# Layer 1's lead maxima: from six after each gate product, in three banks, to four ahead of each half of one, in four banks

## The chip, the cores and the metric

The kernel runs on one core of one Trainium2 chip. The metric is the device time of one execution in microseconds; the number compared is the median over runs.

## The reference

Two layers act on 1024 latent tokens and 256 context tokens with model width 1024. Layer 0 is grouped-query attention, layer 1 is multi-head latent attention with 16 heads. Each layer projects its input, attends, multiplies the result by a gate and projects back. The change touches layer 1 alone, in which the context tokens give keys but no output:

```python
def mla_attend(q_nope, q_rope, k_nope, k_rope, v):
    s = (jnp.einsum('bqhd,bkhd->bhqk', q_nope, k_nope)
         + jnp.einsum('bqhr,bkr->bhqk', q_rope, k_rope)).astype(jnp.float32) * ((MLA_NOPE + MLA_ROPE) ** -0.5)
    p = jax.nn.softmax(s, axis=-1).astype(v.dtype)
    return jnp.einsum('bhqk,bkhd->bqhd', p, v)
...
    o = sweep_query_blocks(lambda qn, qr: mla_attend(qn, qr, kn_all, kr_all, v_all), q_nope, q_rope)
    y = (o.reshape(B, S, MLA_WIDTH) * jax.nn.silu(g)) @ p["w_out"]
```

`g`, the gate, is 1024 columns of the product `h @ w_in`. A softmax needs, for each query, the maximum of its scores (or a number near it) before the exponentials are taken.

## The kernel before

All products run on TensorE in 32-bit floats, with each operand split in a high and a low part, so that one product is three matmuls (`mm3`: lines 94, 95 and 96).

**The gate slices.** The gate is made transposed, in slices of 128 columns by 512 tokens (`gate_slice`). A slice is 8 steps of the contraction times 3, so 24 matmuls of 128x512 into one bank of PSUM (a tile `mm` of the pool `ps_mm`, which has four). ScalarE then takes a tanh of the bank into a tile `gth` (line 303; the pool `wkg1` has two such tiles), VectorE makes the gate of both (line 304), and SyncE stores it to DRAM (line 305, `sgd<-gth`). The last eight slices of layer 1 stand in a loop of their own just ahead of the attention. They are called slices 0 to 7 here; slice 7 is made as two halves of 256 tokens.

**The maxima.** A unit is one head. For a unit the kernel computes, from the high parts alone, the scores of each 128 queries against 512 latent keys (kind `lat`, 16 to a unit) or of twice 128 queries against the 256 context keys (kind `ctx`, 4 to a unit). Each of these 20 steps takes one bank of PSUM (tile `mx`), which VectorE reduces to a row maximum in `m` (lines 394 and 403). TensorE uses 64 of its 128 rows for such a product: queries 0 to 511 of a head and a copy of its keys lie on partitions 0 to 63 (half 0), queries 512 to 1023 on partitions 64 to 127 (half 1). A `lat` step is two matmuls of 64x512, `KH,QH` and `KR,QR` (line 392); a `ctx` step is four of 64x256 (line 402). The list of steps alternates between the halves, and `side_by_side` issues the parts of two steps in turn. After a unit's 20th step `do_shift` takes the maximum of its three (line 450), and a "turn" transposes it on TensorE (line 459), copies it to `crow` (VectorE, line 461) and sends it by DMA into a row of `QS`, which is an operand of the unit's scores.

**The lead.** Attention's loop (`run`) issues two maxima steps with each tile of scores, but the first 24 are to be there before it starts: all 20 of unit 0 and 4 of unit 1. They are issued in the loop of the gate slices, six after each of the slices 3, 4, 5 and 6. `start_unit` issues the loads of a head (`KH`, `QH`, `QR`, then `KL`, `QL`, `QS`) on SyncE's one queue, on which the stores of the gate stand too.

**What sets the order.** Around these slices a scheduler orders TensorE's instructions. It may move a maximum among the matmuls of a slice that stands later. In `run` the order is that of the code (`manual_schedule`). VectorE, ScalarE, GpSimdE and SyncE are ordered by the scheduler in the loop of the slices, before and after the change; each then runs its list strictly in that order. The `mx` tiles come from a pool `ps_m` of three banks, which is opened before the loop and stays through the attention.

```python
            if 2 < at.step < len(todo_g) - 1:
                at.maxima(at.done + 6, 2)
            at.step += 1
            at.run_turns()
```

Of the kernel before, what the change touches and what calls it, by code (L numbers as in the profile page):

```python
# [10 lines left out]
F32 = mybir.dt.float32  # L11
# [4 lines left out]
AX = mybir.AxisListType  # L16
PSUM = bass.MemoryType.PSUM
DRAM = bass.MemoryType.DRAM

P = 128  # L20
D = 1024
KT = D // P
# [6 lines left out]
HALVES = (True, True)  # L29
WIDE = (True, False)  # L30
# [7 lines left out]
def hybrid_kernel(ctx: ExitStack, tc: tile.TileContext, ins: dict, out: bass.AP):  # L38
    nc = tc.nc
    pe, act, dve, pool, sp = nc.tensor, nc.scalar, nc.vector, nc.gpsimd, nc.sync  # L40
# [49 lines left out]
    def mm3(ps, lh, ll, rh, rl, ks, first=True, last=True, between=None):  # L90

        ks = list(ks)
        for i, k in enumerate(ks):
            pe.matmul(ps, lhsT=lh(k), rhs=rh(k), start=first and i == 0, stop=False)  # L94
            pe.matmul(ps, lhsT=lh(k), rhs=rl(k), start=False, stop=False)  # L95
            pe.matmul(ps, lhsT=ll(k), rhs=rh(k), start=False, stop=last and i == len(ks) - 1)  # L96
            if between is not None:
                between(i)
# [192 lines left out]
            pad(tiles, 96)  # L291
        return tiles.tile([P, KT, n], F32R, name="hh"), tiles.tile([P, KT, n], F32R, name="hl")

    def gate_slice(l, c, m, s0, n, w, hT, ps_mm, wk):

        hh, hl = hT[0 if s0 < NL else 1]
        hs = slice(s0 % NL, s0 % NL + n)
        ms = slice(m * P, (m + 1) * P)
        ps = ps_mm.tile([P, 512], F32, name="mm", tag="mm")
        mm3(ps[:, :n], lambda k: w[0][:, k, ms], lambda k: w[1][:, k, ms],  # L300
            lambda k: hh[:, k, hs], lambda k: hl[:, k, hs], range(KT))
        th = wk.tile([P, 512], F32, name="gth", tag="w512")
        act.activation(th[:, :n], ps[:, :n], AF.Tanh, scale=0.5)
        dve.scalar_tensor_tensor(th[:, :n], th[:, :n], 1.0, ps[:, :n], op0=ALU.add, op1=ALU.mult)  # L304
        sp.dma_start(sgd[l][4 * c + m, :, s0:s0 + n], th[:, :n])
# [4 lines left out]
    class Attention:  # L310
# [15 lines left out]
        def open_early(self, st):  # L326

            l = self.l
            self.kp = st.enter_context(tc.tile_pool(name=f"kp{l}", bufs=self.ops["kbufs"], side="right", reuse_waits="tile"))
            self.qp = st.enter_context(tc.tile_pool(name=f"qp{l}", bufs=self.ops["qbufs"], side="right", reuse_waits="tile"))  # L330
            self.ps_m = st.enter_context(tc.tile_pool(name=f"psm{l}", bufs=2 if WIDE[l] or not HALVES[l] else 3, space=PSUM, side="right", reuse_waits="tile"))
            if HALVES[l]:
                self.ops["open"](self, st)

        def open_late(self, st, stp):
            l = self.l
# [36 lines left out]
                              rhs=s["mk"][:, NL:NT], start=True, stop=True)  # L373
                dve.reduce_max(s["m"][:, 2 * i:2 * i + 2, 2 if u["kind"] == "lat" else 0], m.rearrange("p (a b) -> p a b", a=2), axis=AX.X)

        def max_parts(self, u, step):

            s = self.state[id(u)]
            kind, i, n = step
            if kind == "lat":  # L380
                half, spans = i // 4, [(i % 4, slice(n * 512, n * 512 + 512), slice(0, 512))]
            else:
                half, spans = i // 2, [(2 * (i % 2) + a, slice(NL, NT), slice(a * 256, a * 256 + 256)) for a in range(2)]
            held = {}

            def part(j):
                if j == 0:
                    held["m"] = self.ps_m.tile([P, 512], F32, name="mx", tag="mx")
                pairs = self.ops["maxima"](s, half)
                q, k = pairs[j]  # L390
                for t, ks, cs in spans:
                    pe.matmul(held["m"][:, cs], lhsT=q[:, t * P:(t + 1) * P], rhs=k[:, ks], start=j == 0, stop=j == len(pairs) - 1)  # L392
                if j == len(pairs) - 1:
                    dve.reduce_max(s["m"][:, i, n:n + 1], held["m"], axis=AX.X)  # L394

            def part_ctx():
                held["m"] = self.ps_m.tile([P, 512], F32, name="mx", tag="mx")
                m = held["m"]
                pairs = self.ops["maxima"](s, half)
                for t, ks, cs in spans:  # L400
                    for j, (q, k) in enumerate(pairs):
                        pe.matmul(m[:, cs], lhsT=q[:, t * P:(t + 1) * P], rhs=k[:, ks], start=j == 0, stop=j == len(pairs) - 1)  # L402
                dve.reduce_max(s["m"][:, 2 * i:2 * i + 2, 2 if u["kind"] == "lat" else 0],
                               m.rearrange("p (a b) -> p a b", a=2), axis=AX.X)

            if kind == "ctx":
                return half, [part_ctx] + [lambda: None] * (self.ops["mparts"] - 1)
            return half, [lambda j=j: part(j) for j in range(self.ops["mparts"])]

        def wide_max(self, u, step):  # L410
# [78 lines left out]
                self.todo += [(u, ("ctx", i, 0)) for i in range(4)]  # L489
            self.started += 1  # L490

        def next_maxima(self, upto, limit):

            steps = []
            while self.done < upto:
                if not self.todo and self.started < min(limit, len(self.units)):
                    self.start_unit()
                if not self.todo:
                    break
                u, m = self.todo.pop(0)  # L500
                self.done += 1
                if WIDE[self.l]:
                    steps += enumerate(self.wide_max(u, m))
                    continue
                half, parts = self.max_parts(u, m)
                if m[:2] == ("ctx", 3):
                    parts.append(lambda u=u: self.do_shift(u))
                steps.append((half, parts))
            return steps
# [9 lines left out]
        def maxima(self, upto, limit):  # L519

            if HALVES[self.l]:
                steps = self.next_maxima(upto, limit)
                self.side_by_side(*([f for half, parts in steps if half == a for f in parts] for a in range(2)))
                return
            while self.done < upto:
                if not self.todo and self.started < min(limit, len(self.units)):
                    self.start_unit()
                if not self.todo:
                    break
                u, m = self.todo.pop(0)  # L530
                self.done += 1
                self.do_max(u, m)
                if m[:2] == ("ctx", 3):
                    self.do_shift(u)
# [320 lines left out]
    ps_mm = stP.enter_context(tc.tile_pool(name="psmm0", bufs=4, space=PSUM, reuse_waits="tile"))  # L855
# [3 lines left out]
    right = dict(side="right", reuse_waits="tile")  # L859
    lat = st0.enter_context(tc.tile_pool(name="hlat0", bufs=1, reuse_waits="tile"))  # L860
    pad(lat, 96)
    hT = [(lat.tile([P, KT, NL], F32R, name="hh"), lat.tile([P, KT, NL], F32R, name="hl")), None]
# [5 lines left out]
    wk = stR.enter_context(tc.tile_pool(name="wk0", bufs=6, **right))  # L868
# [264 lines left out]
    parts = [[ModPart(0, sec, q, 256, lambda: mp[0], 4, wk, ps_mod, ps_tp) for q in range(4)] for sec in range(2)]  # L1133
# [246 lines left out]
    at = Attention(0, units, dict(scale=0.125, load=l0_load, scores=l0_scores, maxima=l0_maxima, mparts=1, open=l0_open, gaps=(4, 8, 11), kbufs=2, qbufs=3, vw=256))  # L1380
    stE = ExitStack()
# [6 lines left out]
    pieces = []  # L1388
# [36 lines left out]
    ps_mm = stP.enter_context(tc.tile_pool(name="psmm1", bufs=4, **rpsum))  # L1425
# [27 lines left out]
    with ExitStack() as st:  # L1453
        xp = st.enter_context(tc.tile_pool(name="xpp0", bufs=4, **right))
        gp = st.enter_context(tc.tile_pool(name="gp0", bufs=1, **right))
        wk = st.enter_context(tc.tile_pool(name="wk1a", bufs=3, **right))
# [46 lines left out]
    hT = hT1  # L1503
# [4 lines left out]
    with ExitStack() as st:  # L1508
        wk = st.enter_context(tc.tile_pool(name="wk1b", bufs=6, **right))
# [174 lines left out]
    for p_ in range(8):  # L1684
        for par in range(2):
# [3 lines left out]
    at = Attention(1, units, dict(scale=float(96 ** -0.5), load=l1_load, scores=l1_scores, maxima=l1_maxima, mparts=2, open=l1_open, gaps=(4, 6, 9),  # L1689
                                  kbufs=3, qbufs=3, vw=128))  # L1690
    stE = ExitStack()

    with ExitStack() as st:
        wk = st.enter_context(tc.tile_pool(name="wk1c", bufs=8, **right))
# [93 lines left out]
        wg = load_weight(w_in1, KT, 672, 512)  # L1788
# [15 lines left out]
        todo_g = list(slices)  # L1804
        staged(range(TL), q_compress, q_latent, later, expand(0), gate((0, 0, 0, 0, 0, 1, 1, 1)), later, store(0))
        wqb.append(load_weight(ins["l1_w_q_b"], 3, 768, 768))
        wg1 = load_weight(w_in1, KT, 1184, 512)
# [4 lines left out]
    pieces = []  # L1812
    wo = [load_weight(ins["l1_w_out"], KT, 0, 512, 0, todo=pieces)]
    with tc.tile_pool(name="wkg1", bufs=2 if HALVES[1] else 4, **right) as wkg:
        at.start_unit()
        todo_g = [(0, *v) for v in todo_g] + [(1, *v) for v in slices]
        for c, m, s0 in todo_g:
            for s1, n in ((s0, 256), (s0 + 256, 256)) if (c, m, s0) == todo_g[-1] else ((s0, 512),):
                gate_slice(1, c, m, s1, n, (wg, wg1)[c], hT, ps_mm, wkg)
            if 2 < at.step < len(todo_g) - 1:  # L1820
                at.maxima(at.done + 6, 2)
            at.step += 1
            at.run_turns()
            if at.step % 2 == 0:
                pieces.pop(0)()()
    stP.close()
    stl.close()


# [62 lines left out]
```

## Time and profile before

| | |
|---|---|
| median of 3 runs | 1680.79 us (1679.54 to 1683.7) |
| profiled execution, its own time | 1686.67 us |
| its span, first to last instruction | 1684.9 us |
| granted TensorE clock, mean | 0.996 |
| TensorE matmuls busy | 1648.9 us, 98% of the span |
| VectorE busy | 1046.5 us, 62% |
| ScalarE busy | 640.7 us, 38% |
| GpSimdE busy | 950.6 us, 56% |

In the profile's views PE is TensorE (PEld its weight loads), DVE VectorE, ACT ScalarE, POOL GpSimdE, and SPq the queue on which SyncE issues DMAs. A row of the timeline gives the start of an instruction, its duration, engine, source line, what it writes and reads, and how many like it were merged (x2 with one start: two that run side by side, or one just behind the other). A bracket at its end says how long the engine had been idle, and what released it. Matmuls are pipelined: each lasts about 0.39 us, while the next one starts 0.23 us after it, so what a matmul costs is read from the distance between starts.

### The profile page before, as it was taken

The page shows a single profiled execution, that of the slowest core. Times are in us where ns is not written, and L with a number is a line of the kernel's source. Part 1 is how long each engine was busy: PE and PEld are TensorE (multiplying, and loading weights), DVE is VectorE, ACT ScalarE, POOL GpSimd, SP SyncE. Part 2 cuts the span into 40 slices and gives each one's busy share as a digit, 9 for nine tenths or more (in the row PEclk, how much of TensorE's full clock was granted, in tenths as well). Part 3 has the DMA queues.
Part 4 walks back from the last instruction along what each step waited for, and adds up shares of the span by engine and source line. Part 5 has one row for each costly group of instructions (what it writes and reads, how often), then busy time and mean ns, then how long its engine had stood idle before and what let it go on. Part 6 is the DMA issues. An engine that isn't in the chain of part 4 may idle for free. (4 is left out here: it accounts for less than half of the span.)

```text
span 1684.9 us, 27275 instructions
## 1 busy us (share of the span) xinstructions
PE 1648.9 (98%) x10236; PEld 1194.2 (71%) x10236; DVE 1046.5 (62%) x1660; ACT 640.7 (38%) x944; POOL 950.6 (56%) x624
## 2 busy tenths in 40 slices
PE   7999999999999999999989999999999999999998
PEld 5776768875555555468878798886766767767587
DVE  3774553457788877526575657744777777677231
ACT  3642222225454554433244633330534434334310
POOL 2673441118899898833245645450668778777521
PEclk9999999999999999999999999999999999999999
DMA  8548856532352422256324857776566555653451
GB/s 290 194 126 254 253 163 197 156 91 58 83 138 77 126 74 72 79 156 186 125 81 137 241 166 195 222 207 150 127 139 141 133 131 120 133 134 81 121 172 70
DMA packets 221116, 244.21 MB, mean 145 GB/s; under 512 B 23160, under 2 KB 160616, under 8 KB 220984
## 3 DMA queue, kind: packets, MB, share of 16 engines
q1 hardware_dynamic: 220560, 242.36, 51.7%
q8 instruction: 81, 1.33, 0.4%
q14 instruction: 51, 0.42, 0.1%
q10 hardware_dynamic: 424, 0.11, 0.0%
HBM read 168.62 MB, written 73.63 MB: 144 GB/s over the span
## 5 line engine op out<-in xcount | busy, mean ns | idle before, releaser
L552 ACT ACTIVATE p<-st 128x1024 f32<-128x1024 f32 x328 | 335.9, 1027 | 156.9 <-PE st L545 143.2
L586 POOL TENSOR_TENSOR acp<-acp,p 128x1024 f32<-128x1024 f32 x128 | 305.2, 2384 | 8.3 <-ACT p L552 0.4
L394 DVE TENSOR_REDUCE m<-mx 128x1 f32<-128x512 f32 x256 | 176.2, 691 | 94.0 <-PE mx L392 88.1
L430 DVE TENSOR_REDUCE m<-mx 128x1 f32<-128x1024 f32 x128 | 150.4, 1220 | 68.9 <-PE mx L421 68.4
L586 POOL TENSOR_TENSOR acp<-p 128x1024 f32<-128x1024 f32 x34 | 81.5, 2399 | 185.5 <-ACT p L552 185.3
L602 PE MATMUL avt<-p,v 128*64 128x512 f32 x672 | 152.6, 598 | 0.6 <-DVE crow L461 0.3
L586 POOL TENSOR_TENSOR acp<-acp,acd 128x1024 f32<-128x1024 f32 x60 | 142.0, 2366 | 14.6 <-DVE acd L572 11.2
L572 DVE TENSOR_REDUCE acd<-p 128x512 f32<-128x1024 f32 x124 | 144.7, 1220 | 6.9 <-ACT p L552 6.9
L602 PE MATMUL av<-p,v 128*64 128x512 f32 x640 | 141.1, 595 | 0.0
L137 POOL TENSOR_TENSOR wb<-wraw,wa 128x512 fp32r<-128x512 f32 (+3 forms) x65 | 88.4, 1374 | 82.2 <-ACT wa L158 82.2
L94 PE MATMUL mm<-wa,hh 128*128 128x512 f32 (+2 forms) x336 | 127.6, 380 | 1.1 <-ACT hh L959 1.1
L96 PE MATMUL mm<-wa,hl 128*128 128x512 f32 (+2 forms) x336 | 122.0, 363 | 1.5 <-DVE hl L962 1.5
L545 PE MATMUL st<-QH,KH 64*128 64x512 f32 x320 | 122.2, 407 | 0.6 <-DVE gth L304 0.5
L95 PE MATMUL mm<-wb,hh 128*128 128x512 f32 (+2 forms) x336 | 121.3, 361 | 0.0
L545 PE MATMUL st<-QH,KL 64*128 64x512 f32 x320 | 117.7, 391 | 0.0
L545 PE MATMUL st<-QL,KH 64*128 64x512 f32 x320 | 117.2, 390 | 0.0
L94 PE MATMUL y<-wa,oh 128*128 128x512 f32 (+1 forms) x296 | 114.1, 385 | 0.6 <-ACT oh L798 0.6
L95 PE MATMUL y<-wb,oh 128*128 128x512 f32 (+1 forms) x296 | 113.5, 384 | 0.0
L96 PE MATMUL y<-wa,ol 128*128 128x512 f32 (+1 forms) x296 | 113.5, 384 | 0.0
L602 PEld LDWEIGHTS av<-p,v 128*64 128x64 f32 x640 | 44.4, 137 | 88.3 <-issue 87.6
L602 PEld LDWEIGHTS avt<-p,v 128*64 128x64 f32 x672 | 44.9, 136 | 86.9 <-issue 80.6
L94 PE MATMUL mm<-hh,wa 128*128 128x512 f32 (+1 forms) x264 | 103.2, 391 | 0.1
(247 smaller groups left out, 4039.2 us busy)
## 6 DMA issues: line engine op xcount, KB each, us to landing
mraw<-in_l_w_mod SPq DMA_DIRECT2D x64, 256.0 KB
wraw<-in_l_w_in SPq DMA_DIRECT2D x28, 512.0 KB
KH<-k1h SPq DMA_DIRECT2D x32, 320.0 KB
KL<-k1l SPq DMA_DIRECT2D x32, 320.0 KB
rb<-rrow SPq DMA_DIRECT2D x72, 128.0 KB
mraw<-in_l_w_mod SPq DMA_DIRECT2D x16, 512.0 KB
QA<-q0h SPq DMA_DIRECT2D x32, 256.0 KB
wraw<-in_l_w_out SPq DMA_DIRECT2D x16, 512.0 KB
```

Of the source, the lines that this page charges most:

```text
L94: pe.matmul(ps, lhsT=lh(k), rhs=rh(k), start=first and i == 0, stop=False)
L95: pe.matmul(ps, lhsT=lh(k), rhs=rl(k), start=False, stop=False)
L96: pe.matmul(ps, lhsT=ll(k), rhs=rh(k), start=False, stop=last and i == len(ks) - 1)
L137: eng.tensor_sub(lo, a, b)
L394: dve.reduce_max(s["m"][:, i, n:n + 1], held["m"], axis=AX.X)
L430: dve.reduce_max(s["m"][:, i, 0:1], m, axis=AX.X)
L545: pe.matmul(ps[:, n * 512:(n + 1) * 512], lhsT=lh, rhs=rh, start=j == 0, stop=j == last)
L552: act.activation(p, ps, AF.Exp, scale=self.ops["scale"])
L572: dve.reduce_sum(t[:, ns], p2.rearrange("p a n -> p n a")[:, ns, :], axis=AX.X)
L586: pool.tensor_add(t, a, b)
L602: pe.matmul(s["av"][64 * n:64 * n + 64, :], lhsT=s["v"][:, kt, u["vc"]:u["vc"] + 64], rhs=p[:, n * 512:(n + 1) * 512], start=kt == kts[0], ...
```

## The change

Three things change together.

- The lead moves. Four steps are issued at each of two places of a slice: ahead of its first matmul, and after its 12th. This is done for slices 4, 5 and 6, so six times four, again 24.
- TensorE's order in this loop is that of the code (`manual_schedule` on that engine), where the scheduler had set it.
- The lead has a pool of its own with four banks, which is closed after the loop; the pool of three banks for the attention is opened then.

A `ctx` step is cut in its four matmuls, so that `side_by_side` alternates between the halves matmul by matmul in these too. In the attention's loop they stay whole. The instructions are otherwise the same in number and kind.

```diff
-    def gate_slice(l, c, m, s0, n, w, hT, ps_mm, wk):
+    def gate_slice(l, c, m, s0, n, w, hT, ps_mm, wk, between={}):
...
-        mm3(ps[:, :n], lambda k: w[0][:, k, ms], lambda k: w[1][:, k, ms],
-            lambda k: hh[:, k, hs], lambda k: hl[:, k, hs], range(KT))
+        for k0 in range(0, KT, KT // 2):
+            between.get(k0, lambda: None)()
+            mm3(ps[:, :n], lambda k: w[0][:, k, ms], lambda k: w[1][:, k, ms],
+                lambda k: hh[:, k, hs], lambda k: hl[:, k, hs], range(k0, k0 + KT // 2), k0 == 0, k0 + KT // 2 == KT)
...
-            self.ps_m = st.enter_context(tc.tile_pool(name=f"psm{l}", bufs=2 if WIDE[l] or not HALVES[l] else 3, space=PSUM, side="right", reuse_waits="tile"))
+            self.lead_room = ExitStack()
+            if WIDE[l]:
+                self.open_maxima(st)
+            else:
+                self.ps_m = self.lead_room.enter_context(tc.tile_pool(name=f"psl{l}", bufs=4, space=PSUM, side="right", reuse_waits="tile"))
...
+        def open_maxima(self, st):
+            l = self.l
+            self.ps_m = st.enter_context(tc.tile_pool(name=f"psm{l}", bufs=2 if WIDE[l] or not HALVES[l] else 3, space=PSUM, side="right", reuse_waits="tile"))
...
-            if 2 < at.step < len(todo_g) - 1:
-                at.maxima(at.done + 6, 2)
-            at.step += 1
...
+        def four_maxima():
+            at.maxima(min(at.done + 4, 24), 2)
+
+        with tc.manual_schedule(engines={mybir.EngineType.PE}):
+            for c, m, s0 in todo_g:
+                for s1, n in ((s0, 256), (s0 + 256, 256)) if (c, m, s0) == todo_g[-1] else ((s0, 512),):
+                    gate_slice(1, c, m, s1, n, (wg, wg1)[c], hT, ps_mm, wkg,
+                               {0: four_maxima, KT // 2: four_maxima} if 3 < at.step < len(todo_g) - 1 else {})
+                at.step += 1
...
     stP.close()
+    at.lead_room.close()
+    at.open_maxima(stE)
```

How the order of the instructions changes is shown at three places. Outside this loop every engine's order is as before. Source lines above 300 stand some lines lower in the changed file: 392 becomes 402, 403 becomes 415, 304 becomes 306, 305 becomes 307.

TensorE, from the last matmul of slice 3 on (`mm` is a gate product, `mx` a maximum). Before:

```order
L96 MATMUL mm<-hh,wb 128x512
L392 MATMUL mx<-KH,QH 128x512 x2
L392 MATMUL mx<-KR,QR 128x512 x2
L392 MATMUL mx<-KH,QH 128x512
L392 MATMUL mx<-KR,QR 128x512
L94 MATMUL mm<-hh,wa 128x512
L392 MATMUL mx<-KH,QH 128x512
L392 MATMUL mx<-KR,QR 128x512
L95 MATMUL mm<-hl,wa 128x512
L392 MATMUL mx<-KH,QH 128x512
L392 MATMUL mx<-KR,QR 128x512
L96 MATMUL mm<-hh,wb 128x512
```

After the change, at the same place:

```order
L96 MATMUL mm<-hh,wb 128x512
L402 MATMUL mx<-KH,QH 128x512 x2
L402 MATMUL mx<-KR,QR 128x512 x2
L402 MATMUL mx<-KH,QH 128x512 x2
L402 MATMUL mx<-KR,QR 128x512 x2
L94 MATMUL mm<-hh,wa 128x512
L95 MATMUL mm<-hl,wa 128x512
```

Before, the first two steps of six go as a pair, the third stands alone, and the other three each stand alone between single gate matmuls. After, two pairs stand together and twelve gate matmuls follow.

VectorE, from the gates of slices 0 to 2 on (`gth` is a gate, `m<-mx` a maximum). Before:

```order
L304 SCALAR_TENSOR_TENSOR gth<-gth,mm 128x512 x3
L394 TENSOR_REDUCE m<-mx 128x1 x6
L304 SCALAR_TENSOR_TENSOR gth<-gth,mm 128x512 x2
L394 TENSOR_REDUCE m<-mx 128x1 x6
L304 SCALAR_TENSOR_TENSOR gth<-gth,mm 128x512
```

After:

```order
L306 SCALAR_TENSOR_TENSOR gth<-gth,mm 128x512 x3
L404 TENSOR_REDUCE m<-mx 128x1 x7
L306 SCALAR_TENSOR_TENSOR gth<-gth,mm 128x512
L404 TENSOR_REDUCE m<-mx 128x1
L306 SCALAR_TENSOR_TENSOR gth<-gth,mm 128x512
L404 TENSOR_REDUCE m<-mx 128x1 x8
L306 SCALAR_TENSOR_TENSOR gth<-gth,mm 128x512
L415 TENSOR_REDUCE m<-mx 128x2 x4
```

The gate of slice 3 stood behind six maxima; now it stands between the seventh and the eighth.

SyncE's queue, from the stores of slices 1 and 2 on; `KH`, `QH`, `QR` and `KL` are loads of unit 1 here. Before:

```order
L305 DMA sgd_96<-gth 128x512 x2
L1631 DMA KH<-k1h 64x1280
L1632 DMA QH<-q1h 64x512
L305 DMA sgd_96<-gth 128x512
L1634 DMA QR<-q1h 32x512 x2
L305 DMA sgd_96<-gth 128x512
L1631 DMA KH<-k1h 64x1280
L1632 DMA QH<-q1h 64x512
L1634 DMA QR<-q1h 32x512 x2
L1641 DMA KL<-k1l 64x1280
```

After:

```order
L307 DMA sgd_96<-gth 128x512 x2
L1646 DMA KH<-k1h 64x1280
L1647 DMA QH<-q1h 64x512
L1649 DMA QR<-q1h 32x512
L307 DMA sgd_96<-gth 128x512
L1649 DMA QR<-q1h 32x512
L1646 DMA KH<-k1h 64x1280
L307 DMA sgd_96<-gth 128x512
L1647 DMA QH<-q1h 64x512
L1649 DMA QR<-q1h 32x512 x2
L1656 DMA KL<-k1l 64x1280
```

The stores of slices 3 and 4 change places with a load or two; the last load that unit 1's first maximum needs still stands behind both.

More of the change, by code (lines that the diff above doesn't have):

```diff
@@ L374, in do_max, with max_parts @@
                 dve.reduce_max(s["m"][:, 2 * i:2 * i + 2, 2 if u["kind"] == "lat" else 0], m.rearrange("p (a b) -> p a b", a=2), axis=AX.X)
-        def max_parts(self, u, step):
+        def max_parts(self, u, step, fine):
             s = self.state[id(u)]
@@ L394, in part, with part_ctx @@
                     dve.reduce_max(s["m"][:, i, n:n + 1], held["m"], axis=AX.X)
-            def part_ctx():
-                held["m"] = self.ps_m.tile([P, 512], F32, name="mx", tag="mx")
+            def part_ctx(j):
+                if j == 0:
+                    held["m"] = self.ps_m.tile([P, 512], F32, name="mx", tag="mx")
                 m = held["m"]
                 pairs = self.ops["maxima"](s, half)
[L400 to L404, printed above, removed]
+                (t, ks, cs), (q, k) = spans[j // len(pairs)], pairs[j % len(pairs)]
+                pe.matmul(m[:, cs], lhsT=q[:, t * P:(t + 1) * P], rhs=k[:, ks], start=j % len(pairs) == 0,
+                          stop=j % len(pairs) == len(pairs) - 1)
+                if j == len(spans) * len(pairs) - 1:
+                    dve.reduce_max(s["m"][:, 2 * i:2 * i + 2, 2 if u["kind"] == "lat" else 0],
+                                   m.rearrange("p (a b) -> p a b", a=2), axis=AX.X)
             if kind == "ctx":
-                return half, [part_ctx] + [lambda: None] * (self.ops["mparts"] - 1)
+                n_ctx = len(spans) * self.ops["mparts"]
+                if fine:
+                    return half, [lambda j=j: part_ctx(j) for j in range(n_ctx)]
+                return half, [lambda: [part_ctx(j) for j in range(n_ctx)]] + [lambda: None] * (self.ops["mparts"] - 1)
             return half, [lambda j=j: part(j) for j in range(self.ops["mparts"])]
@@ L490, in start_unit, with next_maxima @@
             self.started += 1
-        def next_maxima(self, upto, limit):
+        def next_maxima(self, upto, limit, fine=False):
             steps = []
@@ L504, in next_maxima @@
                     continue
-                half, parts = self.max_parts(u, m)
+                half, parts = self.max_parts(u, m, fine)
                 if m[:2] == ("ctx", 3):
@@ L521, in maxima @@
             if HALVES[self.l]:
-                steps = self.next_maxima(upto, limit)
+                steps = self.next_maxima(upto, limit, True)
                 self.side_by_side(*([f for half, parts in steps if half == a for f in parts] for a in range(2)))
@@ L1816, in hybrid_kernel @@
         todo_g = [(0, *v) for v in todo_g] + [(1, *v) for v in slices]
-        for c, m, s0 in todo_g:
-            for s1, n in ((s0, 256), (s0 + 256, 256)) if (c, m, s0) == todo_g[-1] else ((s0, 512),):
-                gate_slice(1, c, m, s1, n, (wg, wg1)[c], hT, ps_mm, wkg)
-            if 2 < at.step < len(todo_g) - 1:
-                at.maxima(at.done + 6, 2)
-            at.step += 1
-            at.run_turns()
-            if at.step % 2 == 0:
-                pieces.pop(0)()()
+        def four_maxima():
[6 more added lines that the diff above has]
+                at.step += 1
+                at.run_turns()
+                if at.step % 2 == 0:
+                    pieces.pop(0)()()
     stP.close()
+    at.lead_room.close()
+    at.open_maxima(stE)
     stl.close()
```

## The prediction

> **What bounds the kernel now.** I read the page's head first, then the busy time by stretch, then who TensorE (PE) waits for, then the timelines of the loop that is changed.
>
> ```profile
> span 1684.9 us, 27275 instructions
> PE 1648.9 (98%) x10236; PEld 1194.2 (71%) x10236; DVE 1046.5 (62%) x1660; ACT 640.7 (38%) x944; POOL 950.6 (56%) x624
> ...
> 1138.00:1177.00 39.00, 38.69 (x180) 26.05 (x178) 18.64 (x31) 3.15 (x6) 0.00 (x0) 1.00 0.60 152
> 1177.00:1197.00 20.00, 19.49 (x163) 16.63 (x164) 17.03 (x26) 10.28 (x11) 11.98 (x6) 1.00 0.65 173
> 1197.00:1600.00 403.00, 402.91 (x2998) 272.74 (x2995) 275.16 (x397) 170.05 (x177) 296.45 (x143) 1.00 0.53 124
> ...
> PE st L545 <- DVE gth L304: 0.5, 1, 0.5
> ...
> 1177.52 0.49 PE L545 MATMUL st<-QH,KH 64*128 64x512 f32 x1 [0.51 <-DVE gth L304]
> ```
>
> The stretches give busy time of PE, PEld, DVE, ACT, POOL, then clock, DMA share and GB/s. The changed loop is 1138 to 1177: PE is busy 38.69 of 39 us at full clock. From 1177 to the end the only wait of PE on another engine is the one in the last two rows, 0.5 us, at the attention's first score. So PE is the bound in the loop and behind it, and what PE saves in the loop ought to arrive at the end. A busy PE need not do useful work, though: whether matmuls run side by side is seen in the distances between starts.
>
> ```profile
> 1137.70 0.39 PE L95 MATMUL mm<-hl,wa 128*128 128x512 f32 x1
> 1137.92 0.39 PE L96 MATMUL mm<-hh,wb 128*128 128x512 f32 x1
> 1138.24 0.50 PE L392 MATMUL mx<-KH,QH 64*128 64x512 f32 x2
> 1138.58 0.75 PE L392 MATMUL mx<-KR,QR 64*128 64x512 f32 x2
> 1138.87 0.49 PE L392 MATMUL mx<-KH,QH 64*128 64x512 f32 x1
> ...
> 1139.53 0.50 PE L94 MATMUL mm<-hh,wa 128*128 128x512 f32 x1
> 1139.96 0.49 PE L392 MATMUL mx<-KH,QH 64*128 64x512 f32 x1
> 1140.29 0.39 PE L392 MATMUL mx<-KR,QR 64*128 64x512 f32 x1
> 1140.62 0.50 PE L95 MATMUL mm<-hl,wa 128*128 128x512 f32 x1
> ...
> 1142.80 0.50 PE L94 MATMUL mm<-hh,wa 128*128 128x512 f32 x1
> 1143.14 0.40 PE L95 MATMUL mm<-hl,wa 128*128 128x512 f32 x1
> ...
> 1147.78 0.50 PE L392 MATMUL mx<-KH,QH 64*128 64x512 f32 x2
> 1148.12 0.40 PE L392 MATMUL mx<-KR,QR 64*128 64x512 f32 x2
> 1148.35 0.39 PE L392 MATMUL mx<-KH,QH 64*128 64x512 f32 x1
> ...
> 1176.19 0.28 PE L95 MATMUL mm<-hl,wa 128*128 128x256 f32 x1
> 1176.31 0.28 PE L96 MATMUL mm<-hh,wb 128*128 128x256 f32 x1
> ```
>
> Two gate matmuls follow each other by 0.227 us (1137.70 to 1137.92, rounded), of 256 columns by 0.12. Going from 128 rows to 64 takes 0.32 (1137.92 to 1138.24); going back takes 0.33 (1140.29 to 1140.62); the first step behind a switch is slow too, 0.34 (1142.80 to 1143.14). But a pair of both halves takes one step: two `KR,QR` at 1148.12, the next at 1148.35, so 0.23 for two.
>
> **The sum on PE.** I count from slice 3's last matmul (1137.92) to slice 7's (1176.31): 38.39 us. Bare gate products would take 73 steps of 0.227 and 47 of 0.12, 22.2 us. The 24 maxima, the turn and all stalls thus cost 16.2 us now, 0.67 each. A lone one between gate matmuls costs 0.86: from L94 at 1139.53 to L95 at 1140.62 are 1.09, less 0.227.
>
> After the change, four stand together: 0.32 to enter, 0.34, 0.23 and 0.23 between the four rows of pairs, 0.33 to leave, 0.34 for the first gate matmul's step; less two gate steps of 0.227 that would be there anyhow, 1.34 us. For the group of context maxima the rows of 256 columns stand for the step:
>
> ```profile
> 1166.60 0.40 PE L402 MATMUL mx<-KH,QH 64*128 64x256 f32 x2
> 1166.82 0.29 PE L402 MATMUL mx<-KR,QR 64*128 64x256 f32 x2
> 1166.93 0.29 PE L402 MATMUL mx<-KH,QH 64*128 64x256 f32 x2
> ...
> 1167.17 0.39 PE L392 MATMUL mx<-KH,QH 64*128 64x512 f32 x1
> ...
> 1171.77 0.28 PE L95 MATMUL mm<-hl,wa 128*128 128x256 f32 x1
> 1171.89 0.27 PE L459 MATMUL mx<-ident,m 128*8 128x128 f32 x1
> 1171.91 0.36 PE L96 MATMUL mm<-hh,wb 128*128 128x256 f32 x1
> ```
>
> Eight rows of pairs: 0.32 to enter, 0.22, six times 0.115, about 0.2 to leave and 0.33, less 0.45: 1.3 us. Six groups make 8.0 us. The turn is moved from within slice 7 to its front; it puts some 0.1 us between two products, as it did. In all 8.1 against 16.2, a gain of 8.1 us if nothing waits anew; call it 8.0, since the first pairs of the loop ran a little slower (1138.58 to 1138.87, 0.29). What could be off in it is the leaving of a pair of 512 columns, which no row of this loop shows: between 0.23 (no loss) and 0.66 (as if the pair's two came one behind the other), so from +0.5 to -1.7 us over five groups. I take 0.33, the lone product's, since a pair's rows already stand at the spacing of one.
>
> **New waits.** Four banks turn over each half slice, 1.34 + 12 x 0.227 = 4.07 us. What frees a bank is DVE:
>
> ```profile
> 1139.01 2.48 DVE L394 TENSOR_REDUCE m<-mx 128x1 f32<-128x512 f32 x4 [4.78 <-PE mx L392]
> ...
> 1146.24 0.69 DVE L304 SCALAR_TENSOR_TENSOR gth<-gth,mm 128x512 f32<-128x512 f32 x1 [2.65 <-ACT gth L303]
> ...
> 1145.61 0.60 ACT L303 ACTIVATE gth<-mm 128x512 f32<-128x512 f32 x1 [12.11 <-DMA sgd<-gth]
> ```
>
> Four reductions take 2.48 us and a gate 0.69: 3.2 us at most in 4.07, so DVE keeps up on average. At one place it doesn't. Slice 3's tanh starts at 1145.61 only, because its `gth` tile waits for an old store to land; that is before the loop's middle and comes from DMAs that don't move. In the new list of DVE its gate (1146.24 to 1146.93) stands ahead of the eighth maximum, which so ends at about 1147.5. Slice 5's second pair wants that bank: slice 4 ends its matmuls 2 x 4.07 after 1137.92, at 1146.06, and that pair would come at 1146.06 + 0.32 + 0.57 = 1146.95. It starts at 1147.6, 0.65 late, and 0.1 goes with the restart. From below nothing (the store lands half a microsecond sooner); from above 1.4, if the `QR` load that now stands ahead in SyncE's queue delays the landing. I take 0.75.
>
> The Trainium skill, page TensorEngine Tiling (Array Packing), section PSUM Bottleneck, says that packing makes TensorE faster but not the emptying of PSUM, which may then become the bound. By that rule every group would wait for its banks as the third does, which is the second case of the first rival; the trace's 2.48 and 0.69 in 4.07 speak against it so far.
>
> So slice 5 ends its matmuls at 1146.06 + 8.14 + 0.75 = 1154.95, slice 6 at 1163.1, and slice 7, a turn and 47 steps of 0.12 later, at 1169.1. At the other groups: group 4 starts at 1151.2, and its banks are free at 1150.5 (slice 4's gate to 1148.0, then 2.48). Group 6's second pair comes at 1154.95 + 0.32 + 4.06 + 0.57 = 1159.9; its bank is free at 1159.2 (tanh 0.6 and gate 0.69 of slice 5 to 1156.7, then four context maxima). Both have 0.7 us to spare.
>
> **Loads of unit 1.** Its first maximum moves from 1167.17 to about 1159.3. Its last `QR` stands in SyncE's queue behind the gates of slices 3 and 4:
>
> ```profile
> 1138.65 0.84 SPq L305 DMA_DIRECT2D sgd<-gth  x2
> ...
> 1149.23 0.34 SPq L305 DMA_DIRECT2D sgd<-gth  x1
> 1149.62 0.45 SPq L1631 DMA_DIRECT2D KH<-k1h  x1
> 1150.11 0.60 SPq L1632 DMA_DIRECT2D QH<-q1h  x1
> 1150.76 1.05 SPq L1634 DMA_DIRECT2D QR<-q1h  x2
> ```
>
> Now issued by 1151.8; after, slice 4's store goes at about 1148.3 and the last `QR` by 1150.5. The slowest landing here is the store issued at 1138.65 which ends ACT's wait at 1145.6, 7 us behind a full queue. Even 7 us make 1157.5, before 1159.3. Cost nothing, margin 1.8 us.
>
> **The handover.** The turn follows slice 6, at about 1163.3, so 5.8 us ahead of the last gate matmul (1169.1), where it was 4.4 ahead (1171.89 to 1176.31). The two halves of slice 7 write their tanh into tiles from which slices 5 and 6 are stored, at 1156.8 and, by the same steps, 1164.9; the second is wanted at 1169.4, 4.5 us later.
>
> ```profile
> 1146.96 0.33 SPq L305 DMA_DIRECT2D sgd<-gth  x1
> ...
> 1147.00:1150.00 3.00, 3.00 (x14) 1.72 (x12) 1.48 (x3) 0.60 (x1) 0.00 (x0) 1.00 0.40 131
> ```
>
> With an empty queue, a store (128x512 floats, 262 KB) and the two `QR` behind it (131 KB) are through in 3 us: 131 GB/s for 3 us are 393 KB. So 4.5 suffices, by 1.5. The first score still waits for slice 7's gate, the 0.5 of the last waits row. The fourth bank goes back to the attention's scores; its last reduction stands ahead of slice 7, some 5 us of matmuls earlier.
>
> In all 8.0 - 0.75 = 7.3 us. The profiled execution took 1686.67 us around its span of 1684.9, which is 5.9 above the median of 1680.79. Against its own time the sum says 1679.4; against the median, which I predict, 1673.5.
>
> **Rivals.** (1) *The gain is half eaten in the loop*: pairs don't run as one in the written order, or banks come free late at each group. If each row of a pair took 0.46 rather than 0.23, four rows of 512 in five groups and eight of 256 in one add 5.5 us; then 1679. If instead every group waited the 0.65 + 0.1 that I see at one, 3.75 more, 1677.3. The row at 1148.12 speaks against the first, 2.48 in 4.07 against the second. Chance 0.14.
> (2) *The change doesn't do what it says at the end*: the attention takes its start from something else than PE (the `QS` row, a `gth` store, the first `v`), and the gain turns into a wait: 1680.8. The 0.5 us as the only wait behind the loop speaks against it; a view of before can't show a wait that was hidden by 7 us. Chance 0.05.
> (3) *Slower*: in the written order PE can't pass by unit 1's first maximum, and its `KH`, `QH` and `QR` come late; before, the gate matmuls of slice 7 could fill in. To cost the gain they would have to land after 1159.3 + 7.3 = 1166.6, and to be slower by 0.3% after 1171.6; that is 21 us after issue, three times the slowest landing shown. Landing at 1173 gives 1680.8 + 6.4 = 1687. Chance 0.03.
>
> **The numbers.** The forecast, 1671 to 1676, has 0.78. A difference below 0.3% (5 us) can't be told from none here: the three runs alone spread over 4.2 us. The forecast lies 2.2 us past that bound, and a median moves by a microsecond or two, so both cases of the first rival and the second rival count as no change. Faster 0.78, same 0.19, slower 0.03. For the range I take +0.5 of the leaving step, no stall and a microsecond and a half of drift below (1670), the worst of the leaving step, of the stall and half of rival 1 above (1678.5).
>
> **What would show it.** In the changed kernel's timeline: rows of pairs 0.23 apart in groups of four, a slice with maxima 8.1 us long; one wait of about 0.6 us of PE on a maximum of DVE at the third group, none at the sixth; the first score at about 1170 in place of 1177.5, and every later stage earlier by as much. Pairs 0.46 apart, a wait at each group, or a wait of the first scores on a DMA would prove me wrong.

## The result, and the profile after

| | median | runs | ratio to before, 95% interval |
|---|---|---|---|
| before | 1682.76 us | 7 | |
| after | 1674.2 us | 7 | 0.9959 [0.9948, 0.997] |
| before, with the first set of experiments | 1682.02 us | 25 | |
| before, with the second set of experiments | 1681.89 us | 10 | |
| after, measured again with the second set | 1674.88 us | 5 | 0.9965 [0.9951, 0.9978] |

One of the seven runs of before took 1823.73 us: it counts in the median, not in the ratio. By the two intervals the changed kernel is 0.2 to 0.5% faster, some 7 us. The profiled execution of after took 1679.43 us around a span of 1677.6; that of before 1686.67 around 1684.9. So the two traces are 7.3 us apart, and each is some 4 to 5 us above its own median.

From the changed kernel: the page's head, the busy time by stretch, and the one wait of PE on another engine behind the loop's start, in the table of waits and in the timeline.

```profile
span 1677.6 us, 27271 instructions
PE 1643.1 (98%) x10236; PEld 1192.1 (71%) x10236; DVE 1047.3 (62%) x1660; ACT 640.9 (38%) x944; POOL 950.0 (57%) x624
...
1138.00:1170.00 32.00, 31.93 (x182) 23.99 (x180) 18.40 (x32) 3.16 (x6) 0.00 (x0) 1.00 0.73 186
1170.00:1190.00 20.00, 19.56 (x162) 16.68 (x164) 17.04 (x26) 10.27 (x10) 12.02 (x6) 1.00 0.64 172
1190.00:1592.00 402.00, 401.89 (x2995) 271.36 (x2992) 275.12 (x397) 170.03 (x177) 296.56 (x143) 1.00 0.54 124
...
PE st L560 <- DVE gth L306: 0.5, 1, 0.5
...
1170.44 0.50 PE L560 MATMUL st<-QH,KH 64*128 64x512 f32 x1 [0.51 <-DVE gth L306]
```

The loop's work (some 180 matmuls) fits in 32 us where it took 39, at the same granted clock of 1.00, and PE is "busy" for nearly all of it in both kernels. Busy time hides what changed; the starts show it. These are PE's rows at the first two groups of maxima, at a later one, and at the loop's end:

```profile
1138.41 0.39 PE L96 MATMUL mm<-hh,wb 128*128 128x512 f32 x1
1138.73 0.50 PE L402 MATMUL mx<-KH,QH 64*128 64x512 f32 x2
1139.07 0.70 PE L402 MATMUL mx<-KR,QR 64*128 64x512 f32 x2
1139.31 0.70 PE L402 MATMUL mx<-KH,QH 64*128 64x512 f32 x2
1139.64 0.59 PE L402 MATMUL mx<-KR,QR 64*128 64x512 f32 x2
1140.17 0.50 PE L94 MATMUL mm<-hh,wa 128*128 128x512 f32 x1
...
1142.79 0.39 PE L96 MATMUL mm<-hh,wb 128*128 128x512 f32 x1
1143.11 0.50 PE L402 MATMUL mx<-KH,QH 64*128 64x512 f32 x2
1143.45 0.40 PE L402 MATMUL mx<-KR,QR 64*128 64x512 f32 x2
1143.68 0.40 PE L402 MATMUL mx<-KH,QH 64*128 64x512 f32 x2
1143.91 0.40 PE L402 MATMUL mx<-KR,QR 64*128 64x512 f32 x2
1144.24 0.50 PE L94 MATMUL mm<-hh,wa 128*128 128x512 f32 x1
...
1147.78 0.40 PE L402 MATMUL mx<-KH,QH 64*128 64x512 f32 x2
...
1169.23 0.28 PE L96 MATMUL mm<-hh,wb 128*128 128x256 f32 x1
```

All maxima now stand as x2, two halves at once, four rows behind one another (eight in the group of context maxima). The first group takes 4.38 us with its twelve gate matmuls (1138.41 to 1142.79), the second 4.10 (to 1146.89). From slice 3's last matmul to slice 7's are 1169.23 - 1138.41 = 30.82 us, against 38.39 before: 7.57 us less. I call this the loop's length; it is the measure of each experiment below, since it is free of the few microseconds by which whole executions differ. The first score is 7.1 us earlier than before, and the end 7.3.

### The profile page after: what moved, and what is told of

Read it like the earlier page. It is cut to its first block, busy times and chain, and to the rows that moved or that the text cites. A ratio compares the mean times of both kernels' runs of the same rounds, so it can differ in the third digit from the quotient of the medians.

```text
span 1677.6 us, 27271 instructions
## 1 busy us (share of the span) xinstructions
PE 1643.1 (98%) x10236; PEld 1192.1 (71%) x10236; DVE 1047.3 (62%) x1660; ACT 640.9 (38%) x944; POOL 950.0 (57%) x624
```

## The experiments

My theory was that three things are needed together: places in fours (fewer passages between 128 and 64 rows), four banks (so that a pair can start while the pair ahead of it is reduced), and an issue that alternates between the halves. The rivals: that alternate issue does not matter, since TensorE finds the partner by itself; that the banks alone, or the written order alone, bring most of it. The changed kernel gave a loop of 30.82 us, and 31.10 when measured again. Ratios go by the runs of before of the same set: four banks, three banks, in twos and halves belong to the first set, the others to the second. Each loop is that of the one profiled execution.

| kernel | loop, us | median, us | ratio, 95% interval |
|---|---|---|---|
| before | 38.39 | | 1 |
| four banks alone | 35.32 | 1680.46 | 0.9984 [0.9974, 0.9995] |
| written order alone | 46.08 | 1688.49 | 1.0038 [1.0025, 1.0051] |
| after, with three banks | 37.85 | 1681.6 | 0.9994 [0.9985, 1.0004] |
| after, in twos | 32.99 | 1676.75 | 0.9971 [0.9959, 0.9982] |
| after, halves one behind the other | 31.50 | 1677.76 | 0.9973 [0.9963, 0.9984] |
| after, again | 31.10 | 1674.88 | 0.9965 [0.9951, 0.9978] |
| after, other banks at the handover | 31.06 | 1675.8 | 0.9962 [0.995, 0.9975] |
| after, three gate tiles | 31.01 | 1673.93 (one run) | |

**Halves issued one behind the other.** In `maxima`; outside layer 1's loop the order of TensorE's instructions stays what it was:

```diff
-                self.side_by_side(*([f for half, parts in steps if half == a for f in parts] for a in range(2)))
+                for a in range(2):
+                    for half, parts in steps:
+                        if half == a:
+                            for f in parts:
+                                f()
```

> The loop is measured from the start of slice 3's last gate matmul to the start of slice 7's last: 38.4 us before, 30.8 us after the change. This kernel is the changed one, but within each group of four the two steps of half 0 are issued whole, then the two of half 1, in place of turn by turn. My theory: the gain comes mostly from pairs, and a pair runs as one because its matmuls are issued side by side. Then four rows of 64x512 in five groups and eight of 64x256 in one take twice their time: 30.8 + 5.5 = 36.3 us, and 2 us faster than before instead of 7. Rival: TensorE starts a matmul of the free half past one that waits for the other half, so that the order within a group is of no account: 30.8 us and the full gain. The rows of context maxima in the kernel before (issued half by half, yet shown in twos at 1166.60) speak for the rival.

The loop took 31.50 us, so the rival held. The timeline of this kernel, a group of 512 columns and then the group of context maxima:

```profile
1138.78 0.51 PE L402 MATMUL mx<-KH,QH 64*128 64x512 f32 x2
1139.12 0.40 PE L402 MATMUL mx<-KR,QR 64*128 64x512 f32 x2
1139.35 0.40 PE L402 MATMUL mx<-KH,QH 64*128 64x512 f32 x2
...
1151.08 0.38 PE L412 MATMUL mx<-KH,QH 64*128 64x256 f32 x1
1151.30 0.28 PE L412 MATMUL mx<-KR,QR 64*128 64x256 f32 x1
1151.42 0.28 PE L412 MATMUL mx<-KH,QH 64*128 64x256 f32 x1
1151.54 0.28 PE L412 MATMUL mx<-KR,QR 64*128 64x256 f32 x1
1151.65 0.39 PE L412 MATMUL mx<-KH,QH 64*128 64x256 f32 x2
...
1152.01 0.38 PE L412 MATMUL mx<-KR,QR 64*128 64x256 f32 x2
1152.23 0.28 PE L412 MATMUL mx<-KH,QH 64*128 64x256 f32 x1
...
1152.80 0.50 PE L94 MATMUL mm<-hh,wa 128*128 128x512 f32 x1
```

In the 512 groups half 1's first matmul was issued behind four of half 0, and still starts with the first of them: x2 at the same 0.23 spacing. In the context group it was issued behind eight, and starts with half 0's fifth; so four go alone at the front and four at the end, and the group takes 1.72 us (1151.08 to 1152.80) where the changed kernel takes 1.15. In both groups a matmul of half 1 starts beside the one of half 0 that was issued four before it, and not sooner. In the context group no bank held it back, as VectorE had read the four maxima before it by 1150.22. TensorE looks about four matmuls ahead into the other row half, as far as these groups show. Alternating matmul by matmul, rather than eight and eight, is worth 0.57 us there, and alternation within a 512 group nothing. Cutting the context steps in their matmuls is not shown to bring anything: in the kernel before they were issued four and four, and stand in pairs too (the prediction's row at 1166.60). The Trainium skill, page "TensorE: Matmul & The Clock Gate", section "The mechanism" of its part on packing, says that only weight loads are pulled ahead while matmuls start and end strictly in the order of issue. By that rule half 1 could have started beside half 0's last matmul at the earliest: three steps of 0.23 us more in each of five groups and seven of 0.115 in the sixth, some 4.3 us by estimate. The trace does not agree, for two different halves of the rows. The loop is 0.68 us longer than in the changed kernel: this 0.57, and 0.11 in the first group (below). The median is some 3 us above that of after; the intervals overlap, and the rest is not resolved.

**Three banks.**

```diff
-                self.ps_m = self.lead_room.enter_context(tc.tile_pool(name=f"psl{l}", bufs=4, ...))
+                self.ps_m = self.lead_room.enter_context(tc.tile_pool(name=f"psl{l}", bufs=3, ...))
```

> The changed kernel with three banks for the lead instead of four; places and order stay. My theory: the fourth step of each group waits until VectorE has read the first one's bank, 0.77 + 0.69 + 0.05 = 1.5 us after the group's start where it now starts at 0.57. With the slow restart that is 1.0 us for each of six groups: a loop of 37.0 us, a gain of 1.4 us instead of 7.5. Rival, that the written places give the gain and banks don't matter: 30.8 us.

37.85 us: nearly all of the gain is gone. PE's waits in this kernel (us in all, times, longest), a gate on VectorE and PE's row in the third group, and the loop as one stretch (busy PE, PEld, DVE, ACT, POOL, then clock):

```profile
PE mx L402 <- DVE m L404: 3.3, 5, 1.1
PE mx L412 <- DVE m L415: 1.2, 1, 1.2
...
1146.88 0.69 DVE L306 SCALAR_TENSOR_TENSOR gth<-gth,mm 128x512 f32<-128x512 f32 x1 [2.00 <-ACT gth L305]
...
1148.23 0.49 PE L402 MATMUL mx<-KH,QH 64*128 64x512 f32 x1 [1.12 <-DVE m L404]
...
1135.60:1173.45 37.85, 33.31 (x178) 23.91 (x177) 18.72 (x31) 2.77 (x5) 0.00 (x0) 1.00 0.62 162
```

One wait in each of the six groups, 4.5 us in all: the fourth maximum of a group needs the bank of the first, which DVE must have reduced. That is the idle time in the stretch's 33.31 of 37.85. The rest of the 7.0 us would be the pairs around each wait, which run partly alone (the x1 at 1148.23). In four groups the wait is 0.55 us; in the third and the fifth, where DVE makes a gate ahead of the group's first reduction (the row at 1146.88), it is 1.12 and 1.23. The expectation had one price for all six, and so 37.0. So the fourth bank decides, not by itself, but because four steps are issued at once.

**Two steps at four places of a slice in place of four at two.** The same 24 steps, the same banks, twelve excursions into 64 rows in place of six:

```diff
-        for k0 in range(0, KT, KT // 2):
+        for k0 in range(0, KT, KT // 4):
...
-            at.maxima(min(at.done + 4, 24), 2)
+            at.maxima(min(at.done + 2, 24), 2)
...
-                               {0: four_maxima, KT // 2: four_maxima} if 3 < at.step < len(todo_g) - 1 else {})
+                               {k0: four_maxima for k0 in range(0, KT, KT // 4)} if 3 < at.step < len(todo_g) - 1 else {})
```

> The changed kernel with a single pair at each of four places in slices 4, 5 and 6 (before matmuls 1, 7, 13 and 19), twelve pairs instead of six groups of two pairs; four banks. My theory: going from 128 rows to 64 and back costs 0.41 us beyond the work, paid twelve times instead of six: a pair by itself costs 0.32 + 0.34 + 0.33 + 0.34 - 0.45 = 0.88 us, twelve make 10.6 against 8.1, a loop of 33.3 us. Rival, that side by side is all and the change of mode costs nothing: 30.8 us.

32.99 us, and (32.99 - 30.82) / 6 = 0.36 us for an excursion that is saved. It is 0.41, as expected, when the 0.3 us by which the changed kernel's first group is late is left out (next section): this kernel doesn't have it. The timeline of one:

```profile
1143.63 0.40 PE L96 MATMUL mm<-hh,wb 128*128 128x512 f32 x1
1143.96 0.50 PE L402 MATMUL mx<-KH,QH 64*128 64x512 f32 x2
1144.30 0.40 PE L402 MATMUL mx<-KR,QR 64*128 64x512 f32 x2
1144.62 0.50 PE L94 MATMUL mm<-hh,wa 128*128 128x512 f32 x1
1144.96 0.40 PE L95 MATMUL mm<-hl,wa 128*128 128x512 f32 x1
```

Steps of 0.33, 0.34, 0.32 and 0.34, where steps inside a mode are 0.23: about 0.1 more at each of four, and this once more for every excursion. The Trainium skill, page "TensorEngine Tiling (Array Packing)", section "Key Properties", says that a change of the tiling mode drains TensorE, without a price. The trace agrees that it costs something.

**Four banks alone**, in the kernel before: its places and its scheduler's order stay, only the pool of the lead is the changed kernel's.

```diff
-            self.ps_m = st.enter_context(tc.tile_pool(name=f"psm{l}", bufs=2 if WIDE[l] or not HALVES[l] else 3, ...))
+            self.lead_room = ExitStack()
+            if WIDE[l]:
+                self.open_maxima(st)
+            else:
+                self.ps_m = self.lead_room.enter_context(tc.tile_pool(name=f"psl{l}", bufs=4, ...))
```

> The kernel before with one part of the change alone: the lead's pool has four banks and is closed after the loop. Six maxima follow each of slices 3 to 6 as before, in the scheduler's order, which now puts four in pairs and the last two alone. My theory: 1.34 us for the four and twice 0.86 for the others, 3.1 us for six instead of 4.05; four times that makes 12.3 us of maxima and a loop of 34.5 to 35 us, about half the gain. Rival, that the bank alone gives it: 30.8 us; that the places alone give it: 38.4 us.

35.32 us, a little over the 34.5 to 35 written, and 3.1 of the 7.6 gained. The scheduler now finds a bank for a whole pair more often, but six steps at one place are still more than four banks. In the first three of the four groups the fifth and sixth step run alone, in the second and third among the gate matmuls:

```profile
1147.02 0.49 PE L400 MATMUL mx<-KH,QH 64*128 64x512 f32 x1 [0.22 <-DVE m L402]
```

**The written order alone**, in the kernel before: its loop under `manual_schedule`, with six steps after each slice and three banks.

```diff
-        for c, m, s0 in todo_g:
...
+        with tc.manual_schedule(engines={mybir.EngineType.PE}):
+            for c, m, s0 in todo_g:
...
```

> The kernel before with TensorE's order in the loop taken from the code and nothing else: six maxima at once behind each of slices 3 to 6, three banks. My theory: banks decide; the fourth, fifth and sixth of each six wait for VectorE (the fourth from 0.57 to 1.5 us as with three banks in groups of four, the sixth to 2.7), so six cost some 3.6 us for 4.05 before, and the turn, now right behind the last six, waits some 2 us for the reductions: a loop of 37.5 to 39.5 us against 38.4 before, no gain. Rival, that the written order gives the gain: 31 to 34 us.

46.08 us, where 37.5 to 39.5 had been written: missed. Of this kernel: PE's waits, the loop as one stretch and its slowest 6 us (columns as above), and two gate matmuls in them.

```profile
PE mx L392 <- DVE m L394: 3.2, 5, 1.1
PE mx L392 <- DVE m L403: 1.0, 2, 0.7
...
1135.34:1181.42 46.08, 41.88 (x179) 30.33 (x177) 18.45 (x31) 2.77 (x5) 0.00 (x0) 0.81 0.50 136
...
1150.00:1156.00 6.00, 6.00 (x15) 4.29 (x16) 1.59 (x3) 0.00 (x0) 0.00 (x0) 0.50 0.67 172
...
1151.50 0.63 PE L95 MATMUL mm<-hl,wa 128*128 128x512 f32 x1
1151.92 0.63 PE L96 MATMUL mm<-hh,wb 128*128 128x512 f32 x1
```

In the first group the waits are as expected: its fourth maximum starts 1.5 us behind its first, its sixth 2.8. All in all PE waits 4.2 us; the turn waits for nothing. What was not expected is the clock: a mean of 0.81 over the loop, 0.50 at worst, where gate matmuls follow each other by 0.42 rather than 0.23. Taken out, the loop would be about 46.08 x 0.81 = 37.3 us, an estimate from below, since the waits don't shrink with the clock. That is near what I had written, and about a microsecond under the kernel before. So the written order brings little without banks and places that suit it, and that the loop came out 7.7 us longer goes with the clock. What brought the clock down is not shown. The profiled execution is the slowest of five, but the fastest of them (1685.54) is still above every run of before beside it (up to 1683.06).

Not tried were the new places with the order left to the scheduler, so what the written order adds in the changed kernel has no price of its own.

**The handover's bank.** The attention's first score waits 0.5 us for the gate of slice 7, as its tile lies in the banks that held `mm`. Opening the two pools in the other order gives it two banks of which neither held the second half of slice 7:

```diff
-            for name in (("ps_s",) if WIDE[l] else ("ps_s", "ps_o"), ("ps_o", "ps_s"))[l]:
+            for name in (("ps_s",) if WIDE[l] else ("ps_s", "ps_o"), ("ps_s", "ps_o"))[l]:
```

> The changed kernel with the two PSUM pools of the attention opened in the other order, so that the first tile of scores lies on banks 0 and 1 and not on 1 and 2, of which bank 2 holds the last half slice of the gate. My theory: the first score then waits for the last but one gate alone, which is long done; it starts about 0.3 us behind the last gate matmul's successor instead of 1.2 us behind the last gate matmul with a wait of 0.5, and all that follows comes 0.7 us sooner: 1673.5 where the change has 1674.2, which the times can't resolve but the trace shows. Rival: the second tile of scores, which now gets bank 2, waits instead and the end stays where it was.

The wait is gone. In this kernel's timeline, the loop's last matmul and the first score:

```profile
1164.23 0.28 PE L96 MATMUL mm<-hh,wb 128*128 128x256 f32 x1
...
1164.44 0.49 PE L560 MATMUL st<-QH,KH 64*128 64x512 f32 x1
```

They are 0.21 us apart, 1.21 in the changed kernel. Of this 1.0 us, 0.6 or more are left at the end: from the loop's last matmul to the end of the span are 1671.9 - 1164.23 = 507.7 us, against 508.4 (1677.6 - 1169.23) in the changed kernel; the nine traces with the old order of pools, this one among them, lie at 508.3 to 508.6. In time, 1675.8 against 1674.88 for after on the same chip, that cannot be told from nothing, so this version is not shown to be better.

**A third gate tile.** In the pool `wkg1` two became three, so that slice 3's tanh needs no old store to land.

```diff
-    with tc.tile_pool(name="wkg1", bufs=2 if HALVES[1] else 4, **right) as wkg:
+    with tc.tile_pool(name="wkg1", bufs=3 if HALVES[1] else 4, **right) as wkg:
```

> The changed kernel with three tiles for the gate's tanh in place of two. My theory: slice 3's tanh no longer waits for slice 1's store to land and starts about 0.5 us after slice 3's last matmul has started, instead of 6.8 us; the wait that I predicted at the third group can't arise. Since the changed kernel's trace shows no wait there either, the loop keeps its 30.8 us. Rival: the store's landing holds TensorE up unseen, and the loop gets shorter by some tenths or more.

Slice 3's tanh starts 0.42 us behind the loop's start (6.77 in the changed kernel), and the loop is 31.01 us, the same. The late store is real, and holds nothing up.

**After, again**, beside these on the same chip:

> The changed kernel once more, beside the others of this call and for a second trace. My theory: a loop of 30.8 us again, no wait of TensorE on a reduction in it, a time some 7 us below the kernel before. The first group of four, 0.3 us longer than the others in the first trace, should be so again if it waits for the last load of unit 0, and not if that was chance.

Loop 31.10 us, 1674.88 us; the result stands.

## Why the prediction was right

**The main term.** Written as 8.0 us gained less 0.75 for a stall, 7.25. Measured: 7.57 in the loop, 7.3 in the span, 7.0 and 8.6 between medians. The median forecast was 1673.5, measured 1674.2 and 1674.88. That 7.25 lies so near to 7.57 is in part luck: the main term brought 0.4 us less than 8.0, and the stall of 0.75 did not come, which offset each other.

**Pairs run as one.** Rows of pairs 0.23 apart in groups of four, as the row at 1148.12 of before said. A group takes 4.10 with its gate matmuls; I had 4.07. The step that no row of before showed, leaving a pair of 512 columns, is 0.33 (1143.91 to 1144.24), the value taken. The three-bank and in-twos kernels price two parts of the term, which don't add up: the fourth bank 7.0 us with four steps at once, an excursion 0.36 to 0.41.

**The first group, taken too small.** The prediction gave 0.1 us for slower first pairs. The group takes 0.3 us longer than the others in the changed kernel (4.38 against 4.10), and 0.4 to 0.6 longer in the four other profiles with this placement and four banks, which is why their loops are 31.0 us and more. The weight loads (PEld) of the changed kernel; its last two `QR` loads of unit 0 on SP's queue; and, last, the same loads in the three-bank kernel:

```profile
1138.84 0.19 PEld L402 LDWEIGHTS mx<-KR,QR 64*128 64x128 f32 x1
1139.27 0.18 PEld L402 LDWEIGHTS mx<-KR,QR 64*128 64x128 f32 x1 [0.25 <-issue]
...
1134.52 1.04 SPq L1649 DMA_DIRECT2D QR<-q1h  x2
...
1130.21 1.05 SPq L1649 DMA_DIRECT2D QR<-q1h  x2
```

One half's load of `QR` comes 0.43 us behind the other's. That fits a wait for the last `QR` load of unit 0, and the ten traces bear it out. In seven of them, the kernel before among them, these two loads go out 3.7 to 4.2 us ahead of the loop's start (1134.52 against 1138.41 here), and the first group's `KR,QR` rows come late. In the three others (three banks, in twos, written order) they go out 5.4 to 5.6 us ahead (1130.21 against 1135.60), and the first group is as fast as the rest. No row names the wait, so it stays an inference, though a firm one.

**The stall, mis-sized: 0.75 taken, 0 measured.** The mechanism was there (a gate in DVE's list ahead of the eighth maximum), the moment was not. ACT, DVE and SP's queue in the changed kernel:

```profile
1139.24 0.84 SPq L307 DMA_DIRECT2D sgd<-gth  x2
...
1145.18 0.60 ACT L305 ACTIVATE gth<-mm 128x512 f32<-128x512 f32 x1 [11.18 <-DVE m L404]
...
1145.81 0.69 DVE L306 SCALAR_TENSOR_TENSOR gth<-gth,mm 128x512 f32<-128x512 f32 x1
1146.41 0.68 DVE L404 TENSOR_REDUCE m<-mx 128x1 f32<-128x512 f32 x1
...
1149.52 1.05 SPq L1649 DMA_DIRECT2D QR<-q1h  x2
```

I took the landing of the store from one sample, 6.96 us behind its issue (1138.65 to 1145.61). Here it is 5.94 (1139.24 to 1145.18), and in seven other traces 5.65 to 6.78. The bracket of this tanh names a reduction of DVE; but with a third `gth` tile the tanh comes at 0.42, so it waited for its tile. The eighth maximum ends at 1147.09, and the pair that wants its bank starts at 1147.78, with 0.7 in hand. My lower end had "the store lands half a microsecond sooner"; counted from the loop's start, the tanh came 0.9 sooner (6.77 for 7.69). The late first group gave the pair 0.3 of what it had in hand here; in the kernel measured again it gave 0.58 of 0.65, so that there the stall was missed by less than 0.1. What a gate ahead of a maximum costs when the bank is wanted at once is seen in the three-bank kernel, at another gate, that of slice 4: the wait of 1.12 above, against 0.55 in that kernel's first group.

**The margins.** Groups 4 and 6 and the loads of unit 1 were said to hold by 0.7 and 1.8 us. No wait shows at any of them; the last `QR` goes out by 1150.57 (written: 1150.5) and unit 1's first maximum starts at 1159.50 (written: 1159.3). The turn comes at 1163.50 (1163.3).

**The rivals.** Half eaten in the loop, a handover that waits, loads that come late: none happened. The rule of the Trainium skill (page "TensorEngine Tiling (Array Packing)", section "PSUM Bottleneck") that emptying PSUM may become the bound is borne out one bank lower: with three banks every group waits, with four none does.

## What to carry to other kernels

When products on half the array share a queue with full ones, price a group by the distances between starts (enter, spacing of a pair, leave), not by busy time: the spacing of a pair already in the trace gave the gain to within half a microsecond. Give such a group as many banks as it issues steps at once, and no more steps than banks: here the fourth bank alone brought 3.1 us of 7.6, the new places and order with three banks 0.5. A wait forecast from one landing of a DMA needs the spread of that landing, since a microsecond here was the whole term.

## What the runs showed of the hardware

- TensorE started a matmul of the free row half beside the one of the other half that was issued four before it, in groups of 4 and 4 as in the one of 8 and 8. So interleaving by hand paid only where a half's run was longer than four: 0.57 us in the one such group.
- The granted clock fell to half in the kernel with the written order alone, though PE never waited more than 1.1 us at once; it waited 4.2 us in all, seven times in four groups. The three-bank kernel waited 4.5 us in all, up to 1.2 at once, six times in six groups, and kept 1.00 over its loop. The Trainium skill, page "TensorE: Matmul & The Clock Gate", section "A second HAM failure mode: psum-queue depth-cycling", says that short waits for banks, often enough, throttle the clock; the first trace agrees, and the second shows that a similar total does not always do it. What decides between them stays open.
